# Two edits in a hybrid trunk kernel: a shorter ring of weight operands during the pooling branch, and decays and k ahead of the masked copies in the recurrence

## The chip, the cores and the metric

The kernel runs on one core of one Trainium2 chip. The metric is device time in microseconds (us). Five engines run side by side, each through its own queue in order: TensorE (PE; its weight loads are listed apart as PEld), VectorE (DVE), ScalarE (ACT), GpSimd (POOL) and SyncE (SP, which issues DMAs).

## The reference, cut to what matters

One layer over 2048 tokens of width 1024. The normalised input is projected; one part of the columns goes through a pooling mixer, one through a gated linear recurrence (HGRN2) with 4 heads of 128, both are projected, gated and merged, and a convolved, gated feed-forward layer follows.

```python
def hgrn2_mixer(zq, zf, zi, zo, lb, norm_g):
    q = jax.nn.silu(heads(zq))
    f = lbh + (1.0 - lbh) * jax.nn.sigmoid(heads(zf))
    k = 1.0 - f
    v = heads(zi)
    ...
        b = jnp.cumsum(gc, axis=2)
        diff = b[:, :, :, None, :] - b[:, :, None, :, :]
        decay = jnp.exp(jnp.where(causal[:, :, None], diff, -jnp.inf))
        attn = jnp.einsum('bhtk,bhtsk,bhsk->bhts', qc, decay, kc)
        o = (jnp.einsum('bhts,bhsv->bhtv', attn, vc)
             + jnp.einsum('bhtk,bhkv->bhtv', qc * jnp.exp(b), state))
    ...
xn = rmsnorm(x, norm1_g[l])
z = xn @ w_in[l]
ya = pool_mixer(u_pool, pool_w[l], pool_scale[l]) @ w_pa[l]
yb = hgrn2_mixer(zq, zf, zi, zo, lower_bounds[l], hgrn_norm_g[l]) @ w_pb[l]
x = x + (gates[:, :, 0] * ya + gates[:, :, 1] * yb) @ w_o[l]
x = x + conv_glu_ffn(rmsnorm(x, norm2_g[l]), w_up[l], conv_w[l], conv_b[l], w_down[l])
```

## The kernel before, in words

**Blocks and products.** Tokens are worked in two pairs of blocks of 512, so everything below happens twice: a mixer, then a feed-forward part, for the first 1024 tokens and again for the rest. The large projections use a scheme with seven products P1 to P7 in place of eight. A `Unit` runs them in the order P1, P2, P6, P5, P7, P4, P3 as far as its banks are concerned: P1 and P2 add into PSUM bank X, P6, P7 and P4 into Z, P5 and P3 into V. Between P6 and P7 the partial result in Z has to be read once: that is `u2` (line 1196), a DVE subtraction. P7 may start only when `u2` has read Z; between P7 and P4 stands `u3` (line 1200) in the same way. Each product is computed from operands split into a high and a low part, with three multiplies of 128 x 512 for each 128 rows, all recorded under line 148.

**The weight stream.** `Stream` loads weight tiles ahead (`load`), and `convert` splits one into high (line 231, ACT) and low (line 232, DVE) in a buffer `ops`, one of a ring of `N_OPS` = 6. In the first mixer POOL also forms sums of weight tiles (`comb`, line 444), which are stored and loaded again in the second mixer. `advance` is called once per tick, that is once in six multiplies, and converts the next operand if the program is not too far ahead: neither `room` (4 operands ahead of the one taken last) nor the ring (line 242) may be passed.

**The recurrence.** `hgrn_task` handles one head of one 512-token block; 16 such tasks run, as generators that three runners step forward between the multiplies of the projections. A task works a 128-token square by levels: widths 1 and 2 singly, then `two_levels(4)` and `two_levels(16)` (two widths each), then 64. At a level PE multiplies `k` by masked or scaled copies of `q` (`qm`) into a score bank `pl` (lines 1026 and 1066). DVE copies the valid parts of `pl` into `at` by masked copies (lines 1034 and 1037; 1073 and 1086 at widths 1 and 2), and multiplies `q` (1043), the decays `f` themselves (1045, 1046, 1049) and `k` (1047; 1094 at the single widths) for the next level. `two_levels` handles two halves of the tile, `i` = 0 and 2, each with its own `pl` bank, and one product L1047 scales all of `k`.

**Order.** The kernel emits its program in the order in which the generators step; a scheduler then sets the order on each engine, within the dependencies and the few that the kernel adds (`behind`, `in_turn`). So what stands where on an engine is read from the order of the built program, not from the code alone.

Of the kernel before, what the change touches and what calls it, by code (L numbers as in the profile page):

```python
# [15 lines left out]
ALU = mybir.AluOpType  # L16
AX = mybir.AxisListType

P = 128
# [11 lines left out]
NT = TB // P  # L31
# [44 lines left out]
N_OPS = 6  # L76
# [5 lines left out]
def tile_trunk(  # L82
# [60 lines left out]
    def join(task):  # L143
        while task.live:
            task.step()
# [22 lines left out]
    class Stream:  # L168
        def __init__(self):
            self.raws = []  # L170
            self.ops = []
            self.n_raw = 0
            self.tiles = []
            self.next = 0
            self.done = 0
            self.pins = {}
            self.stop = None
            self.room = LOOKAHEAD

        def raw(self, src, plus=None):  # L180
            r = Raw(src, plus)
# [57 lines left out]
        def advance(self, n):  # L239
            for _ in range(n):  # L240
                j = len(self.tiles)
                if j >= len(self.ops) or j == self.stop or j >= self.next + self.room or j - N_OPS >= self.done:
                    return
                self.convert()

# [34 lines left out]
    stream = Stream()  # L280
# [310 lines left out]
    masks = {}  # L591
# [373 lines left out]
    def hgrn_task(b, h, d, q, vd, zd, od):  # L965
# [23 lines left out]
        def mask(key, n):  # L989
            m = masks[key]  # L990
            return m.unsqueeze(1).to_broadcast([P, n, m.shape[1], m.shape[2]])

        def two_levels(hh):
            nb = P // (4 * hh)
            d5 = d.rearrange("p (c b t h) -> p c b t h", c=NT, t=4, h=hh)
            q5 = q.rearrange("p (c b t h) -> p c b t h", c=NT, t=4, h=hh)
            qv = q.rearrange("p (c b t h) -> p c b t h", c=NT, t=2, h=hh)
            av = att.rearrange("p (c b t h) -> p c b t h", c=NT, t=2, h=hh)
            av2 = att.rearrange("p (c b t h) -> p c b t h", c=NT, t=2, h=2 * hh)
            q2 = q.rearrange("p (c b t h) -> p c b t h", c=NT, t=2, h=2 * hh)  # L1000
            mvs = {}
            for i in range(0, NT, 2):
                cc = slice(i, i + 2)
                mv = (slot(f"qm{b}_{h}_{hh}_{i}")[:, :384]
                      .rearrange("p (c s x) -> p c s x", c=2, s=3))
                near = mv[:, :, 0].rearrange("p c (b h) -> p c b h", h=hh)
                half = mv[:, :, 1].rearrange("p c (b t h) -> p c b t h", t=2, h=hh)
                far = [mv[:, :, 1 + t].rearrange("p c (b h) -> p c b h", h=2 * hh)
                       for t in range(2)]
                act.copy(near, qv[:, cc, :, 1, :])  # L1010
                pool.tensor_copy(half[:, :, :, 0, :], q5[:, cc, :, 2, :])  # L1011
                dve.tensor_tensor(half[:, :, :, 1, :], q5[:, cc, :, 3, :],
                                  d5[:, cc, :, 2, 0:1].to_broadcast([P, 2, nb, hh]), ALU.mult)
                full = [P, 2, nb, 2 * hh]
                dve.tensor_tensor(far[1], far[0], d5[:, cc, :, 1, 0:1].to_broadcast(full),
                                  ALU.mult)
                dve.tensor_tensor(q2[:, cc, :, 1, :], far[1],
                                  d5[:, cc, :, 0, 0:1].to_broadcast(full), ALU.mult)
                mvs[i] = mv
            yield AHEAD  # L1020
            for i in range(0, NT, 2):
                cc = slice(i, i + 2)
                mv = mvs[i]
                pa_ = bank(f"pl{b}_{h}_{hh}_{i}", 384)
                for c in range(2):
                    ins = pe.matmul(pa_[:, c * 192 : c * 192 + 192],  # L1026
                                    ks[:, (i + c) * P : (i + c + 1) * P],
                                    mv[:, c].rearrange("p s x -> p (s x)"),
                                    start=True, stop=True)
                    if not (i or c):  # L1030
                        in_turn(ins)
                ps = pa_.rearrange("p (c s x) -> p c s x", c=2, s=3)
                yield 1
                dve.copy_predicated(av[:, cc, :, 1, :], mask(hh, 2),
                                    ps[:, :, 0].rearrange("p c (b h) -> p c b h", h=hh))
                for t in range(2):
                    dve.copy_predicated(av2[:, cc, :, 1, :], mask(8 * hh + 1 - t, 2),
                                        ps[:, :, 1 + t].rearrange("p c (b h) -> p c b h", h=2 * hh))
            dd = d.rearrange("p (b t h) -> p b t h", t=4, h=hh)
            qq = q.rearrange("p (b t h) -> p b t h", t=4, h=hh)  # L1040
            kk = ks.rearrange("p (b t h) -> p b t h", t=4, h=hh)
            nb *= NT
            dve.tensor_tensor(qq[:, :, 1, :], qq[:, :, 1, :],
                              dd[:, :, 0, 0:1].to_broadcast([P, nb, hh]), ALU.mult)
            dve.tensor_tensor(dd[:, :, 2, 0:1], dd[:, :, 2, 0:1], dd[:, :, 3, 0:1], ALU.mult)
            dve.tensor_tensor(dd[:, :, 1, 0:1], dd[:, :, 1, 0:1], dd[:, :, 2, 0:1], ALU.mult)
            dve.tensor_tensor(kk[:, :, 0:3, :], kk[:, :, 0:3, :],  # L1047
                              dd[:, :, 1:4, 0:1].to_broadcast([P, nb, 3, hh]), ALU.mult)
            dve.tensor_tensor(dd[:, :, 0, 0:1], dd[:, :, 0, 0:1], dd[:, :, 1, 0:1], ALU.mult)

        for lv in (0, 1, 2, 4, 6):
            hh = 1 << lv
            if lv in (2, 4):
                yield from two_levels(hh)
                continue
            nb = P // (2 * hh)
            qv = q.rearrange("p (c b t h) -> p c b t h", c=NT, t=2, h=hh)
            av = att.rearrange("p (c b t h) -> p c b t h", c=NT, t=2, h=hh)
            if lv < 2:
                qd, ad = ((q1, ae), (q2, ao))[lv]  # L1060
                if lv == 1:
                    act.copy(q2[:, :, 0].rearrange("p c (b h) -> p c b h", h=2), qv[:, :, :, 1, :])
                    yield AHEAD
                pa_ = bank(f"pl{b}_{h}_{hh}")
                for c in range(NT):
                    ins = pe.matmul(pa_[:, c * P : (c + 1) * P], ks[:, c * P : (c + 1) * P],
                                    qd[:, c].rearrange("p s x -> p (s x)"),
                                    start=True, stop=True)
                    if not c:
                        in_turn(ins)  # L1070
                yield 2
                pv4 = pa_.rearrange("p (c s x) -> p c s x", c=NT, s=2)
                dve.copy_predicated(ad, masks[-1 - lv].to_broadcast([P, NT, 64]), pv4[:, :, 1])
                pv4 = pv4[:, :, 0].rearrange("p c (b h) -> p c b h", h=hh)
# [10 lines left out]
            if lv < 2:  # L1085
                dve.copy_predicated(av[:, :, :, 1, :], mask(hh, NT), pv4)
            q3 = q.rearrange("p (b t h) -> p b t h", t=2, h=hh)
            k3 = ks.rearrange("p (b t h) -> p b t h", t=2, h=hh)
            d3 = d.rearrange("p (b t h) -> p b t h", t=2, h=hh)
            full = [P, NT * nb, hh]  # L1090
            if lv:
                dve.tensor_tensor(q3[:, :, 1, :], q3[:, :, 1, :],
                                  d3[:, :, 0, 0:1].to_broadcast(full), ALU.mult)
            dve.tensor_tensor(k3[:, :, 0, :], k3[:, :, 0, :],
                              d3[:, :, 1, 0:1].to_broadcast(full), ALU.mult)
            dve.tensor_tensor(d3[:, :, 0, 0:1], d3[:, :, 0, 0:1], d3[:, :, 1, 0:1], ALU.mult)
        yield 4
        pk = bank(f"pk{b}_{h}")
        for c in range(NT):
# [267 lines left out]
    def mixer(b0, forms, late):  # L1367
# [163 lines left out]
                add_forms(two, yf, k, f"yf{b0}", eng=dve)  # L1531

        join(mtask)
        otask = []

        def start_o(n):
# [4 lines left out]
        while any(t.live for t in runners):  # L1541
            for t in runners:
                if t.live:
                    t.step()
        join(otask[0])

        acc = {}

# [329 lines left out]
```

## Time and profile before

| what | value |
|---|---|
| median of 3 runs | 2533.51 us (2533.47 to 2534.64) |
| profiled execution | 2532.39 us |
| its span, first to last instruction | 2530.7 us |
| granted TensorE clock | 0.999 |
| PE busy | 2509.1 us (99%) |
| DVE busy | 1978.5 us (78%) |
| ACT busy | 1176.1 us (46%) |
| POOL busy | 753.4 us (30%) |

Durations in the prediction come from this profiled execution. In a row of the timeline the first number is the start in us from the span's start, the second the duration in us, then engine, line, operation, output and inputs (buffer numbers left out), shapes, and the count of equal rows run together; in brackets stands the idle time before it and what ended that. A row of the waits gives the waiting row, what it waited for, then the sum in us, the times, and the longest. In a row of the groups behind the bar stand the busy time in us and the mean of one in ns.

### The profile page before, as it was taken

How to read it: one execution, taken by the hardware profiler on the slowest of the kernel's cores; microseconds unless marked ns; L12 is line 12 of the kernel's file. 1: busy time of each engine (PE TensorE's matmuls, PEld its weight loads, DVE VectorE, ACT ScalarE, POOL GpSimd, SP SyncE). 2: the span in 40 equal slices, each digit the busy share in tenths (PEclk: the TensorE clock that was granted, in tenths of full speed). 3: DMA queues.
4: the chain of work that ended last, by engine and by line, in shares of the span. 5: the costliest groups of instructions: out<-in, count | busy, mean ns of one | idle time of the engine just before them, and what ended most of it. 6: DMA issues, size and time to landing. Idle time of an engine off the chain costs nothing.

```text
span 2530.7 us, 35649 instructions
## 1 busy us (share of the span) xinstructions
PE 2509.1 (99%) x11508; PEld 2053.6 (81%) x11508; DVE 1978.5 (78%) x3508; ACT 1176.1 (46%) x2218; POOL 753.4 (30%) x1127
## 2 busy tenths in 40 slices
PE   9999999999999999999999999999999999999998
PEld 7888888788888888888888888888888888888886
DVE  7889878598898777885596778765979888778755
ACT  6534343334555454554554343442355554445534
POOL 4344453003354334451320202200033432325410
PEclk9999999999999999999999999999999999999999
DMA  8878777777898879897344343446443454447852
GB/s 270 272 180 233 202 206 231 219 230 244 199 260 228 229 230 241 261 366 243 124 147 150 112 132 108 139 146 225 149 155 117 151 154 135 152 134 245 321 166 97
DMA packets 252332, 493.76 MB, mean 195 GB/s; under 512 B 26544, under 2 KB 43056, under 8 KB 251824
## 3 DMA queue, kind: packets, MB, share of 16 engines
q1 hardware_dynamic: 184512, 313.60, 39.1%
q0 software_dynamic: 42656, 112.74, 17.6%
q10 hardware_dynamic: 24976, 65.13, 7.6%
q8 instruction: 91, 1.49, 0.2%
q14 instruction: 97, 0.79, 0.1%
HBM read 381.79 MB, written 187.17 MB: 225 GB/s over the span
## 4 chain that ended last, share of the span: by engine, by line
PE 91%; DVE 5%; issue 1%; DMA 1%; POOL 1%; ACT 1%; SPq 0%; DVEq 0%; POOLq 0%; ACTq 0%
PE dn_P L148 16%; PE up_Z L148 14%; PE up_X L148 10%; PE up_V L148 10%; PE wo_P L148 6%; PE gr_Z L148 4%; PE pb L148 4%; PE pa L148 3%; PE io_Z L148 3%; PE gr_X L148 3%; PE fr_Z L148 2%; PE gr_V L148 2%; PE io_V L148 2%; PE fr_X L148 2%; PE fr_V L148 2%; PE pl L1026 1%
## 5 line engine op out<-in xcount | busy, mean ns | idle before, releaser
L231 ACT CAST ops<-raw 128x512 fp32r<-128x512 f32 x744 | 459.7, 620 | 817.8 <-PE dn_P L148 177.4
L232 DVE TENSOR_TENSOR ops<-raw,ops 128x512 fp32r<-128x512 f32 x744 | 553.0, 747 | 216.3 <-ACT ops L231 208.4
L1614 DVE SCALAR_TENSOR_TENSOR e<-h,cols,e 128x512 f32<-128x512 f32 x176 | 143.2, 818 | 30.9 <-ACT e L1612 26.3
L1612 ACT ACTIVATE e<-h,cols 128x512 f32<-128x512 f32 x176 | 142.3, 814 | 25.1 <-DVE h L1159 18.2
L1617 DVE SCALAR_TENSOR_TENSOR e<-h,cols,e 128x512 f32<-128x512 f32 x176 | 133.9, 770 | 2.5
L961 POOL DMA_DIRECT2D g_P<-dg_P x154 | 83.8, 545 | 160.3 <-PE dn_P L148 114.1
L1269 POOL TENSOR_TENSOR gf_P<-e,e 128x512 f32<-128x512 f32 x44 | 61.2, 1392 | 150.4 <-DVE e L1623 96.2
L1269 POOL TENSOR_TENSOR gf_P<-gf_P,e 128x512 f32<-128x512 f32 x44 | 59.1, 1344 | 72.0 <-DVE e L1623 71.5
L1409 POOL TENSOR_TENSOR q<-q,qs 128x512 f32<-128x512 f32 x16 | 21.7, 1357 | 185.2 <-ACT qs L1408 178.7
L1607 POOL COPY h<-h 128x2 f32<-128x2 f32 x88 | 40.8, 476 | 117.3 <-DVE h L1158 110.4
L1446 ACT ACTIVATE gt<-gt,cols 128x512 f32<-128x512 f32 x48 | 34.8, 725 | 86.8 <-DVE gt L1159 71.5
L1621 ACT ACTIVATE e<-e 128x512 f32<-128x512 f32 x88 | 55.6, 632 | 38.9 <-DVE e L1617 38.7
L1609 POOL COPY hist<-h 128x2 f32<-128x2 f32 x88 | 35.0, 398 | 117.6 <-DVE h L1159 115.8
L1159 DVE TENSOR_TENSOR h<-up_u,up_V 128x512 f32<-128x512 f32 x88 | 60.0, 682 | 10.2 <-PE up_V L148 9.7
L1244 DVE TENSOR_TENSOR x<-x,wo_P 128x512 f32<-128x512 f32 x88 | 56.0, 680 | 12.1 <-PE wo_P L148 11.9
L1244 DVE TENSOR_TENSOR ac<-ac,dn_P 128x512 f32<-128x512 f32 x72 | 47.1, 681 | 16.7 <-PE dn_P L148 16.5
L1011 POOL COPY qm<-q 128x64 f32<-128x64 f32 x64 | 29.9, 494 | 96.2 <-issue 25.9
L1026 PE MATMUL pl<-qm,k 128*128 128x192 f32 x256 | 50.6, 327 | 3.7 <-DVE k L1047 3.5
L1637 POOL DMA_DIRECT2D dg_P<-gf_P x88 | 50.7, 576 | 8.3 <-POOL gf_P L1269 7.4
L1607 POOL COPY h<-hist 128x2 f32<-128x2 f32 x88 | 45.0, 518 | 27.4 <-DVE m_T42l L657 27.3
L1194 ACT COPY up_e<-up_X 128x512 f32<-128x512 f32 x44 | 25.8, 586 | 58.2 <-PE up_X L148 53.1
L1026 PEld LDWEIGHTS pl<-qm,k 128*128 128x128 f32 x256 | 43.9, 189 | 9.6 <-POOL u L925 2.2
(1285 smaller groups left out, 8088.0 us busy)
## 6 DMA issues: line engine op xcount, KB each, us to landing
g_P<-dg_P POOLq DMA_DIRECT2D x154, 256.0 KB, 6.2
raw<-in_w_up_t SPq DMA_DIRECT2D x132, 256.0 KB, 3.2
raw<-in_w_in_t SPq DMA_DIRECT2D x98, 256.0 KB, 3.5
dg_P<-gf_P POOLq DMA_DIRECT2D x88, 256.0 KB, 4.0
dg_P<-e SPq DMA_DIRECT2D x66, 256.0 KB, 3.6
raw<-in_w_dn SPq DMA_DIRECT2D x66, 256.0 KB, 3.9
x<-in_x SPq DMA_DIRECT2D x64, 256.0 KB, 4.9
gd<-gt ACTq DMA_DIRECT2D x64, 256.0 KB, 3.2
```

The costliest lines, as they stand in the source:

```text
L148: count[1] = pe.matmul(*args, **kw)
L231: self.mark = act.copy(hi, v)
L232: low = self.low = dve.tensor_tensor(lo, v, f32(hi), ALU.subtract)
L961: eng.dma_start(t, d)
L1026: ins = pe.matmul(pa_[:, c * 192 : c * 192 + 192], ks[:, (i + c) * P : (i + c + 1) * P], mv[:, c].rearrange("p s x -> p (s x)"), start=Tru ...
L1159: return dve.tensor_tensor(dst, t, ps, ALU.add if how == "add" else ALU.subtract)
L1244: dve.tensor_tensor(t, t, ps[j], ALU.add if sg > 0 else ALU.subtract)
L1269: pin(eng.tensor_tensor(t, x0, x1, op))
L1607: pool.tensor_copy(h[:, 0:2], hist[:, mt] if hf == 0 else hs[s, 0][:, TB : TB + 2])
L1612: in_turn(act.activation(t, h[:, 2:], AF.Identity, bias=col(o_cb + mt), scale=col(o_cw + 4 * MF + mt)))
L1614: in_turn(second(dve.scalar_tensor_tensor(t, h[:, 1 : 1 + TB], col(o_cw + 2 * MF + mt), t, ALU.mult, ALU.add)))
L1617: dve.scalar_tensor_tensor(t, h[:, 0:TB], col(o_cw + mt), t, ALU.mult, ALU.add)
```

## The change: a shorter ring, and another order in the recurrence

There are two edits. The first makes the ring length a value of the stream and sets it to 5 in place of 6 from the end of the pooling tasks to the end of the pooling branch, with the drain of the recurrences behind it. The second is in `hgrn_task`. In `two_levels` the products of the decays and the remaining `q` product are emitted ahead of the score products, and the `k` product is cut into two halves, one behind each score product and ahead of all masked copies, which come together at the end. At widths 1, 2 and 64 the `k` product comes first, then `q` and the decays, then the masked copies, the larger one ahead of the diagonal one.

```diff
+            self.ring = N_OPS
...
-                if j >= len(self.ops) or j == self.stop or j >= self.next + self.room or j - N_OPS >= self.done:
+                if j >= len(self.ops) or j == self.stop or j >= self.next + self.room or j - self.ring >= self.done:
...
                 mvs[i] = mv
+            dd = d.rearrange("p (b t h) -> p b t h", t=4, h=hh)
+            qq = q.rearrange("p (b t h) -> p b t h", t=4, h=hh)
+            kk = ks.rearrange("p (b t h) -> p b t h", t=4, h=hh)
+            full = [P, NT * nb, hh]
+            dve.tensor_tensor(qq[:, :, 1, :], qq[:, :, 1, :],
+                              dd[:, :, 0, 0:1].to_broadcast(full), ALU.mult)
+            dve.tensor_tensor(dd[:, :, 2, 0:1], dd[:, :, 2, 0:1], dd[:, :, 3, 0:1], ALU.mult)
+            dve.tensor_tensor(dd[:, :, 1, 0:1], dd[:, :, 1, 0:1], dd[:, :, 2, 0:1], ALU.mult)
+            dve.tensor_tensor(dd[:, :, 0, 0:1], dd[:, :, 0, 0:1], dd[:, :, 1, 0:1], ALU.mult)
             yield AHEAD
+            pls = []
             for i in range(0, NT, 2):
...
-                ps = pa_.rearrange("p (c s x) -> p c s x", c=2, s=3)
+                pls.append(pa_.rearrange("p (c s x) -> p c s x", c=2, s=3))
                 yield 1
+                half = slice(i * nb, (i + 2) * nb)
+                dve.tensor_tensor(kk[:, half, 0:3, :], kk[:, half, 0:3, :],
+                                  dd[:, half, 1:4, 0:1].to_broadcast([P, 2 * nb, 3, hh]),
+                                  ALU.mult)
+            for i, ps in zip(range(0, NT, 2), pls):
+                cc = slice(i, i + 2)
                 dve.copy_predicated(av[:, cc, :, 1, :], mask(hh, 2),
                                     ps[:, :, 0].rearrange("p c (b h) -> p c b h", h=hh))
...
-            dve.tensor_tensor(qq[:, :, 1, :], qq[:, :, 1, :],
-                              dd[:, :, 0, 0:1].to_broadcast([P, nb, hh]), ALU.mult)
-            dve.tensor_tensor(dd[:, :, 2, 0:1], dd[:, :, 2, 0:1], dd[:, :, 3, 0:1], ALU.mult)
-            dve.tensor_tensor(dd[:, :, 1, 0:1], dd[:, :, 1, 0:1], dd[:, :, 2, 0:1], ALU.mult)
-            dve.tensor_tensor(kk[:, :, 0:3, :], kk[:, :, 0:3, :],
-                              dd[:, :, 1:4, 0:1].to_broadcast([P, nb, 3, hh]), ALU.mult)
-            dve.tensor_tensor(dd[:, :, 0, 0:1], dd[:, :, 0, 0:1], dd[:, :, 1, 0:1], ALU.mult)
...
-                dve.copy_predicated(ad, masks[-1 - lv].to_broadcast([P, NT, 64]), pv4[:, :, 1])
...
+            dve.tensor_tensor(k3[:, :, 0, :], k3[:, :, 0, :],
+                              d3[:, :, 1, 0:1].to_broadcast(full), ALU.mult)
             if lv:
                 dve.tensor_tensor(q3[:, :, 1, :], q3[:, :, 1, :],
                                   d3[:, :, 0, 0:1].to_broadcast(full), ALU.mult)
-            dve.tensor_tensor(k3[:, :, 0, :], k3[:, :, 0, :],
-                              d3[:, :, 1, 0:1].to_broadcast(full), ALU.mult)
             dve.tensor_tensor(d3[:, :, 0, 0:1], d3[:, :, 0, 0:1], d3[:, :, 1, 0:1], ALU.mult)
+            if lv < 2:
+                pv4 = pa_.rearrange("p (c s x) -> p c s x", c=NT, s=2)
+                dve.copy_predicated(av[:, :, :, 1, :], mask(hh, NT),
+                                    pv4[:, :, 0].rearrange("p c (b h) -> p c b h", h=hh))
+                dve.copy_predicated(ad, masks[-1 - lv].to_broadcast([P, NT, 64]), pv4[:, :, 1])
...
         join(mtask)
+        stream.ring = N_OPS - 1
...
         join(otask[0])
+        stream.ring = N_OPS
```

In the built program DVE has 3483 rows in place of 3451; PE, ACT, POOL and SP have as many as before. In the changed file the lines are shifted: the casts 231 and 232 are 232 and 233, the masked copies 1034 and 1037 are 1050 and 1053, the `q` products 1015, 1017 and 1043 are 1016, 1018 and 1025, the `f` products 1045, 1046 and 1049 are 1027, 1028 and 1029, `k` 1047 is 1045, the score product 1026 is 1036, `u2` 1196 is 1201. In the names the first number is the block of 512 tokens, the second the head, then the width and the half; the last is a count of buffers in the order in which the program made them.

DVE in the first mixer, from the second `k` product of head 0, block 1 to `u2` of unit ur0_0 (site 1 of the prediction), before:

```order
L1047 TENSOR_TENSOR k1_0_1467<-k1_0_1467,f1_0_1436 128x32x12
L232 TENSOR_TENSOR ops48_1780<-raw47_1333,ops48_1780 128x512
L1049 TENSOR_TENSOR f0_0_1390<-f0_0_1390 128x8
L1017 TENSOR_TENSOR q1_0_1364<-qm1_0_16_0_1759,f1_0_1436 128x4x32
L1017 TENSOR_TENSOR q1_0_1364<-qm1_0_16_2_1765,f1_0_1436 128x4x32
L1046 TENSOR_TENSOR f1_0_1436<-f1_0_1436 128x8
L1037 COPY_PREDICATED at0_0_1456<-m32_1036,pl0_0_4_2_1712 128x16x8
L1196 TENSOR_TENSOR ur0_0_u2_1791<-ur0_0_e1_1771,ur0_0_Z_1773 128x512
```

and now:

```order
L1045 TENSOR_TENSOR k1_0_1467<-k1_0_1467,f1_0_1436 128x16x12
L1050 COPY_PREDICATED at1_0_1470<-m4_957,pl1_0_4_2_1722 128x32x4
L1053 COPY_PREDICATED at0_0_1456<-m33_1080,pl0_0_4_2_1718 128x16x8
L1016 TENSOR_TENSOR qm1_0_16_2_1771<-qm1_0_16_2_1771,f1_0_1436 128x2x64
L1027 TENSOR_TENSOR f1_0_1436<-f1_0_1436 128x8
L233 TENSOR_TENSOR ops48_1790<-raw47_1333,ops48_1790 128x512
L1029 TENSOR_TENSOR f0_0_1390<-f0_0_1390 128x8
L1018 TENSOR_TENSOR q1_0_1364<-qm1_0_16_0_1765,f1_0_1436 128x4x32
L1201 TENSOR_TENSOR ur0_0_u2_1801<-ur0_0_e1_1781,ur0_0_Z_1783 128x512
L1053 COPY_PREDICATED at1_0_1470<-m33_1080,pl1_0_4_2_1722 128x16x8
L1053 COPY_PREDICATED at0_0_1456<-m32_1036,pl0_0_4_2_1718 128x16x8
```

The second half of `k1_0` now stands ahead of the copies out of `pl1_0_4_2`. One `q` product, one `f` product and the copy with mask `m32` out of `pl0_0_4_2` have gone from ahead of `u2` to behind it.

PE at the same place, the score products of width 16 of head 0 (`pl`) among the multiplies of unit ur0_0 (bank V is product P5, bank Z is P7), before:

```order
L148 MATMUL ur0_0_V_1793<-x1_T12h_765,ops45_1671 128x512
L1026 MATMUL pl0_0_16_0_1808<-qm0_0_16_0_1739,k0_0_1453 128x192 x2
L148 MATMUL ur0_0_V_1793<-x1_T13h_781,ops45_1671 128x512
L148 MATMUL ur0_0_V_1793<-x1_T13l_782,ops45_1671 128x512
L148 MATMUL ur0_0_V_1793<-x1_T13h_781,ops45_1671 128x512
L1026 MATMUL pl1_0_16_0_1811<-qm1_0_16_0_1759,k1_0_1467 128x192 x2
L1026 MATMUL pl0_0_16_2_1823<-qm0_0_16_2_1745,k0_0_1453 128x192 x2
L1026 MATMUL pl1_0_16_2_1829<-qm1_0_16_2_1765,k1_0_1467 128x192 x2
L148 MATMUL ur0_0_Z_1773<-x1_T30h_827,ops46_1701 128x512
```

and now, where the first `pl` stands three multiplies earlier:

```order
L1036 MATMUL pl1_0_16_0_1821<-qm1_0_16_0_1765,k1_0_1467 128x192 x2
L1036 MATMUL pl0_0_16_2_1831<-qm0_0_16_2_1748,k0_0_1453 128x192 x2
L148 MATMUL ur0_0_Z_1783<-x1_T30h_827,ops46_1709 128x512
L148 MATMUL ur0_0_Z_1783<-x1_T30l_828,ops46_1709 128x512
L148 MATMUL ur0_0_Z_1783<-x1_T30h_827,ops46_1709 128x512
L148 MATMUL ur0_0_Z_1783<-x1_T31h_846,ops46_1709 128x512
L148 MATMUL ur0_0_Z_1783<-x1_T31l_847,ops46_1709 128x512
L148 MATMUL ur0_0_Z_1783<-x1_T31h_846,ops46_1709 128x512
L148 MATMUL ur0_0_Z_1783<-x1_T32h_865,ops46_1709 128x512
L148 MATMUL ur0_0_Z_1783<-x1_T32l_866,ops46_1709 128x512
L1036 MATMUL pl1_0_16_2_1835<-qm1_0_16_2_1771,k1_0_1467 128x192 x2
L148 MATMUL ur0_0_Z_1783<-x1_T32h_865,ops46_1709 128x512
```

The last of the four `pl` groups has moved from ahead of P7 into it, behind eight of its twelve multiplies. PE's order moves at four places in all: here, at unit gr0_6 (there the last group moves the other way, from inside P7 to ahead of it), and by two or three multiplies at units ur2_0 and gr2_6 of the second mixer.

ACT where the ring is shorter, at the seam between the last gate unit and the pooling branch of the first mixer, before:

```order
L231 CAST ops131_4913<-raw97_4601 128x512
L656 CAST mxs1_0h_4816<-mx1_0_4814 128x512
L231 CAST ops132_4937<-raw98_4603 128x512
L1446 ACTIVATE gt0_1_7_4826<-gt0_1_7_4826,cols_84 128x512
L656 CAST mxs1_1h_4844<-mx1_1_4842 128x512
```

and now:

```order
L232 CAST ops131_4929<-raw97_4617 128x512
L657 CAST mxs1_0h_4832<-mx1_0_4830 128x512
L232 CAST ops132_4997<-raw98_4619 128x512
L1451 ACTIVATE gt0_1_7_4842<-gt0_1_7_4842,cols_84 128x512
L657 CAST mxs1_1h_4860<-mx1_1_4858 128x512
```

The program makes operand 132 later (its count grows by 60, its neighbours' by 16), and the cast stands where it stood.

More of the change, by code (lines that the diff above doesn't have):

```diff
@@ L1019, in two_levels @@
                 mvs[i] = mv
+            dd = d.rearrange("p (b t h) -> p b t h", t=4, h=hh)
[7 more added lines that the diff above has]
+            dve.tensor_tensor(dd[:, :, 0, 0:1], dd[:, :, 0, 0:1], dd[:, :, 1, 0:1], ALU.mult)
             yield AHEAD
+            pls = []
             for i in range(0, NT, 2):
-                cc = slice(i, i + 2)
                 mv = mvs[i]
@@ L1038, in two_levels @@
                                         ps[:, :, 1 + t].rearrange("p c (b h) -> p c b h", h=2 * hh))
[L1039 to L1042, printed above, removed]
-            dve.tensor_tensor(qq[:, :, 1, :], qq[:, :, 1, :],
-                              dd[:, :, 0, 0:1].to_broadcast([P, nb, hh]), ALU.mult)
-            dve.tensor_tensor(dd[:, :, 2, 0:1], dd[:, :, 2, 0:1], dd[:, :, 3, 0:1], ALU.mult)
-            dve.tensor_tensor(dd[:, :, 1, 0:1], dd[:, :, 1, 0:1], dd[:, :, 2, 0:1], ALU.mult)
-            dve.tensor_tensor(kk[:, :, 0:3, :], kk[:, :, 0:3, :],
-                              dd[:, :, 1:4, 0:1].to_broadcast([P, nb, 3, hh]), ALU.mult)
-            dve.tensor_tensor(dd[:, :, 0, 0:1], dd[:, :, 0, 0:1], dd[:, :, 1, 0:1], ALU.mult)
         for lv in (0, 1, 2, 4, 6):
@@ L1071, in hgrn_task @@
                 yield 2
-                pv4 = pa_.rearrange("p (c s x) -> p c s x", c=NT, s=2)
-                dve.copy_predicated(ad, masks[-1 - lv].to_broadcast([P, NT, 64]), pv4[:, :, 1])
-                pv4 = pv4[:, :, 0].rearrange("p c (b h) -> p c b h", h=hh)
             else:
@@ L1084, in hgrn_task @@
                 act.copy(av[:hh, :, 0, 1, :], pa_[:hh].rearrange("p (c h) -> p c h", c=NT))
-            if lv < 2:
-                dve.copy_predicated(av[:, :, :, 1, :], mask(hh, NT), pv4)
             q3 = q.rearrange("p (b t h) -> p b t h", t=2, h=hh)
```

## The prediction

> **What bounds the kernel now.** I read the page first (busy shares, the chain that ended last), then what TensorE (PE) waited for in the first mixer, then two stretches side by side, the recurrence of the first and of the second mixer, and last the rows around each PE wait.
>
> ```profile
> span 2530.7 us, 35649 instructions
> PE 2509.1 (99%) x11508; PEld 2053.6 (81%) x11508; DVE 1978.5 (78%) x3508; ACT 1176.1 (46%) x2218; POOL 753.4 (30%) x1127
> PE 91%; DVE 5%; issue 1%; DMA 1%; POOL 1%; ACT 1%; SPq 0%; DVEq 0%; POOLq 0%; ACTq 0%
> PE pl L1026 <- DVE k L1047: 3.5, 2, 1.8
> 118.00:425.00 307.00, 301.56 (x1534) 250.74 (x1533) 271.42 (x635) 120.09 (x276) 134.37 (x143) 1.00 0.80 217
> 1380.00:1680.00 300.00, 299.93 (x1540) 252.20 (x1539) 235.08 (x626) 122.85 (x277) 54.44 (x80) 1.00 0.40 121
> ```
>
> PE is busy 99% of the span and carries 91% of the chain, so the end moves only where PE waits or gets other work. The change adds no PE work. The last two rows (length, then busy time of PE, PEld, DVE, ACT, POOL, then the granted clock) say where a wait can be: in the first mixer's recurrence PE lacks 307.00 - 301.56 = 5.4 us, in the second 300.00 - 299.93 = 0.07 us. The clock is 1.00 in both. In the second the same rows move with the same cover, and I cost them at nothing; if that cover were gone, the prices below would hold there as well. The first row of the waits says what the change can aim at: twice PE's score product `pl` waits for `k` (L1047), 3.5 us together.
>
> **The ring: nothing.** In the order no row stands elsewhere because of it, on any engine, and no row waits for another one; the ACT rows shown above are where it acts, and they keep their places. What it could have touched is this wait at the seam to the pooling branch:
>
> ```profile
> 464.88 1.29 DVE L232 TENSOR_TENSOR ops<-raw,ops 128x512 fp32r<-128x512 f32 x2 [2.58 <-ACT ops L231]
> 466.09 1.12 DVE L1138 SCALAR_TENSOR_TENSOR ot<-po,ro,z 128x128 f32<-128x128 f32 x4
> 466.49 0.33 PE L1144 MATMUL pt<-ident,ot 128*128 128x128 f32 x1 [1.84 <-DVE ot L1138]
> ```
>
> Two weight subtractions (L232) stand ahead of `ot`, and PE waits 1.84 us for `ot`. They still stand there afterwards, so the 1.84 us stay. Cost 0, both ends.
>
> **The decays: prices.** Per pair of levels one `k` product over 384 columns becomes two over 192; 32 rows become 64. Steps are read from starts of rows that follow each other.
>
> ```profile
> L1047 DVE TENSOR_TENSOR k<-k,f 128x384 f32<-128x384 f32 x32 | 19.7, 616 | 0.0
> 154.48 0.48 DVE L1017 TENSOR_TENSOR q<-qm,f 128x128 f32<-128x128 f32 x2
> 154.89 0.16 DVE L1046 TENSOR_TENSOR f<-f 128x8 f32<-128x8 f32 x1
> 154.97 0.28 DVE L1037 COPY_PREDICATED at<-m,pl 128x128 f32<-128x128 uint8 x1
> 155.17 0.67 DVE L1196 TENSOR_TENSOR ur_u<-ur_e,ur_Z 128x512 f32<-128x512 f32 x1
> 158.63 0.54 DVE L1047 TENSOR_TENSOR k<-k,f 128x384 f32<-128x384 f32 x1
> 159.10 0.28 DVE L1034 COPY_PREDICATED at<-m,pl 128x128 f32<-128x128 uint8 x1
> ```
>
> A `q` product of 128 columns steps 0.41 / 2 = 0.20 us, a small `f` product 0.08, a masked copy 0.20, the full `k` 0.47. A half is not in the trace: it lies between 0.20 and 0.47, and on the line through 128 and 384 columns it is 0.27. Two halves cost 0.54 - 0.47 = 0.07 more than a full one, 32 x 0.07 = 2.2 us on DVE in all, hidden where DVE has slack (271 of 307, 235 of 300 us busy). Where it has none, position counts, and there are four such sites. The moved rows issue no DMA, and the rows of POOL and SP keep their order. On ACT three operand copies pass a gate's sigmoid and its store at two places of the second mixer; ACT is busy 122.85 of 300 us there, and no PE wait hangs on it, so that is 0.
>
> **Site 1**, unit ur0_0, the first wait for `k`:
>
> ```profile
> 151.85 0.40 PE L148 MATMUL ur_V<-x_T13h,ops 128*128 128x512 f32 x1
> 154.02 2.26 PE L1026 MATMUL pl<-qm,k 128*128 128x192 f32 x12 [1.77 <-DVE k L1047]
> 155.99 0.53 PE L148 MATMUL ur_Z<-x_T30h,ops 128*128 128x512 f32 x1
> 156.35 0.39 PE L148 MATMUL ur_Z<-x_T30l,ops 128*128 128x512 f32 x1
> 158.92 0.39 PE L148 MATMUL ur_X<-x_f4h,ops 128*128 128x512 f32 x1
> 150.08 1.31 POOL L444 TENSOR_TENSOR w51s<-raw,raw 128x512 f32<-128x512 f32 x1 [1.53 <-issue]
> 151.47 1.51 POOL L444 TENSOR_TENSOR w51s<-w51s,raw 128x512 f32<-128x512 f32 x1
> 150.13 1.29 DVE L1046 TENSOR_TENSOR f<-f 128x8 f32<-128x8 f32 x1
> 151.76 1.26 DVE L1045 TENSOR_TENSOR f<-f 128x8 f32<-128x8 f32 x1
> 153.33 0.55 DVE L1047 TENSOR_TENSOR k<-k,f 128x384 f32<-128x384 f32 x1
> ```
>
> The wait for `k` goes: the halves of `k1_0` stand ahead of the rows that PE then needs, and the first `pl` needs only the first half. But what is late next is already there. Behind the `pl` rows PE starts product P7 (`ur_Z<-x_T30h`, 155.99), which needs `u2` (L1196), and `u2` ran 155.17 + 0.67 = 155.84. It stands in DVE's queue behind all these rows, whichever order they have. After the change a `q` product (0.20), an `f` product (0.08) and a copy (0.20) stand behind it instead of ahead, and two `k` products are halved (+0.14): `u2` is 0.34 earlier. PE's order pays for it: the last `pl` of the four moves into P7 and splits it. Such a group takes 0.56 (414.40 to 414.96, below), and the first multiply behind it 0.36 where others take 0.23 (155.99 to 156.35), together 0.70. So with POOL's holds as they are, site 1 ends 0.70 - 0.34 = 0.36 **later**.
>
> The copies also free the score banks later. The last `pl` group waits for the copy `m32`, which now stands two copies (0.40) behind `u2`; eight multiplies of P7 (8 x 0.23 = 1.8 us) stand ahead of that group and cover it.
>
> The holds are the second half. `f` products of 8 columns took 1.29 and 1.26 us while POOL added weights (L444), 0.16 us otherwise: about 1.1 us lost each time. The new order puts other rows under POOL's sums. I take one hold fewer of the two, 0.36 - 1.1 = -0.74, since the `f` products of this stretch are spread wider; ends +0.36 (both stay) and -1.84 (both missed).
>
> The Trainium skill, "SBUF — State Buffer", section "SBUF: two separate sides", says that VectorE with two SBUF inputs and GpSimd take an exclusive lock for a whole instruction and the loser fully blocks. These rows agree. It also speaks against this change: `k` has two SBUF inputs, a masked copy reads its data from PSUM, so `k` put ahead of copies can hold up rows that would have run on. The trace has such a copy running free under a sum:
>
> ```profile
> 143.28 1.69 POOL L444 TENSOR_TENSOR w46s<-raw,raw 128x512 f32<-128x512 f32 x1 [6.96 <-DMA gd<-gt]
> 143.93 0.29 DVE L1037 COPY_PREDICATED at<-m,pl 128x128 f32<-128x128 uint8 x1
> ```
>
> **Site 2**, unit gr0_6, the second wait:
>
> ```profile
> 410.97 0.89 PE L1026 MATMUL pl<-qm,k 128*128 128x192 f32 x4 [1.77 <-DVE k L1047]
> 414.07 0.50 PE L148 MATMUL gr_Z<-x_T30h,ops 128*128 128x512 f32 x1
> 414.40 0.85 PE L1026 MATMUL pl<-qm,k 128*128 128x192 f32 x4
> 414.96 0.53 PE L148 MATMUL gr_Z<-x_T30l,ops 128*128 128x512 f32 x1
> 417.65 0.40 PE L148 MATMUL gr_X<-x_f4h,ops 128*128 128x512 f32 x1
> 409.12 1.29 POOL L444 TENSOR_TENSOR w121s<-w121s,raw 128x512 f32<-128x512 f32 x1
> 409.19 1.63 DVE L1047 TENSOR_TENSOR k<-k,f 128x384 f32<-128x384 f32 x1
> 413.34 0.67 DVE L1196 TENSOR_TENSOR gr_u<-gr_e,gr_Z 128x512 f32<-128x512 f32 x1
> ```
>
> Again P7 (414.07) starts when `u2` is done (413.34 + 0.67 = 414.01). Ahead of `u2` there are now one copy more (+0.20), one `f` fewer (-0.08) and two halved `k` (+0.14): 0.26 later, P7 at 414.33. Here the order helps PE: the last `pl` group moves from inside P7 to ahead of it, into the wait. P7 took 417.65 - 414.07 = 3.58 with it and takes 3.58 - 0.70 = 2.88 without: it ends at 417.21, -0.44. Ends: -1.5 if the 1.1 us hold on `k` (1.63 against 0.55) is missed, +0.66 if one comes on top.
>
> **Sites 3 and 4**, units gr0_2 and ur0_1, where PE comes to P7 just as `u2` ends or before:
>
> ```profile
> 233.09 0.68 DVE L1196 TENSOR_TENSOR gr_u<-gr_e,gr_Z 128x512 f32<-128x512 f32 x1
> 233.83 0.52 PE L148 MATMUL gr_Z<-x_T30h,ops 128*128 128x512 f32 x1
> 311.29 0.50 PE L148 MATMUL ur_Z<-x_T30h,ops 128*128 128x512 f32 x1 [1.11 <-DVE ur_u L1196]
> ```
>
> At both, three halves stand ahead of `u2` where one full `k` stood: 3 x 0.27 - 0.47 = 0.34 later, each straight onto PE. Ends 0 (a hold that swallows it) and +0.34.
>
> **Sum.** -0.74 - 0.44 + 0.34 + 0.34 = -0.50 us; ends -3.3 and +1.7. The profiled execution took 2532.39 us (span 2530.7, 1.69 around it), the median of the runs is 2533.51, 1.1 above it; I put the difference on the median: 2533.0, with 2530.2 to 2535.2 as its own range.
>
> **The rivals.** *The table is right*: the 3.5 us go and `u2` takes nothing of it. For it: the row of the waits says so. Against it: `u2` ends only 0.15 us and 0.06 us ahead of P7 at the two sites. Time 2533.5 - 3.5 = 2530.0. Chance 0.10.
>
> *Slower by the holds*: `k` ahead of the copies meets one of POOL's sums more at each of the four sites, and `u2` waits behind it. Price per site 1.1 us on the values with holds as today: (0.36 + 1.1) + (-0.44 + 1.1) + 2 x (0.34 + 1.1) = 5.0 us, 2538.5. It decides where a half `k` reaches DVE's head inside a sum while copies stand behind it. For it: the two holds at site 1 and the one at site 2. Against it: the sums start by their own loads and hits fall both ways. Chance 0.08. This is the mechanism on which the skill's rule stands.
>
> *Only half the change exists*: for the ring this is certain from the order and is in the sum; that the decays move nothing is excluded by the rows shown.
>
> **How the numbers follow.** Forecast 0.76, the table 0.10, the holds 0.08, something unseen 0.06, both ways alike. About 0.2% (5.1 us) is what a measurement of this kernel can tell from no change. Faster by that needs more than the whole first row of the waits: 0.03. Slower by that is about half of the second rival and the unseen part: 0.07. The range 2529.8 to 2536.0 takes in the forecast's own ends and the first rival and leaves out the second.
>
> **What would show it.** Right: no `pl <- k` among PE's waits; `u2` (L1201 then) named as what PE waits for at P7 of ur0_0, gr0_6, gr0_2 and ur0_1; `pt <- ot` still 1.8; 64 rows of `k` of 192 columns at about 0.35 us; PE's idle time in the first recurrence near 5 us, in the second under 0.3. Wrong: PE's idle time there under 2.5 us (the table was right), `k` halves of over 1 us in front of `u2` at several sites (the holds), or any new PE wait after 1380 us.

## The result: slower by about 3 us, and the profile after

| | before | changed |
|---|---|---|
| median of 18 runs, us | 2534.67 (2531.84 to 2538.18) | 2537.88 (2535.45 to 2541.02) |
| ratio | 1 | 1.0014, 95% interval 1.0008 to 1.0020 |
| profiled execution, us | 2532.39 | 2539.77 |
| PE idle in 118 to 425 us of the span | 5.4 | 9.3 |

The change costs 3.2 us at the medians, where 0.5 us of gain was forecast. The two profiled executions lie 7.4 us apart: that of before was 2.3 under its median, that of the changed kernel 1.9 over. So the rows below show where the time goes; how much goes there in the mean, the medians say.

The changed kernel's page, span and engines:

```profile
span 2538.0 us, 35650 instructions
PE 2512.8 (99%) x11508; PEld 2054.9 (81%) x11508; DVE 1986.4 (78%) x3540; ACT 1175.4 (46%) x2218; POOL 748.6 (29%) x1127
```

PE is busy 3.7 us longer with as many rows (2509.1 before); the rest of the 7.3 us between the spans is idle time. The windows of the two recurrences, with length and PE's busy time first and the granted clock third from the end:

```profile
118.00:425.00 307.00, 297.70 (x1495) 246.46 (x1494) 270.93 (x631) 117.55 (x270) 130.24 (x144) 0.99 0.77 211
1380.00:1690.00 310.00, 309.93 (x1587) 260.59 (x1586) 242.78 (x651) 128.19 (x287) 59.55 (x84) 1.00 0.40 122
```

The second recurrence is as full as before. Nearly the whole loss lies in the first. PE's lag, the start of a multiply less the start of the same multiply in the trace of before, is 0.5 us at 120 us, 7.0 at 430 and 7.4 at the end. In 118 to 425 us PE now lacks 307.00 - 297.70 = 9.3 us, and its clock is 0.99. What PE waited for there (118 to 470 us, the four largest; total, times, longest):

```profile
PE ur_Z L148 <- DVE ur_u L1201: 3.0, 2, 2.1
PE gr_Z L148 <- DVE gr_u L1201: 1.8, 2, 1.6
PE pl L1036 <- DVE qm L1016: 1.8, 2, 1.1
PE pl L1036 <- DVE at L1053: 1.3, 1, 1.3
```

Both waits for `k` (3.5 us) are gone. In their place PE waits for `u2` (L1201, 4.8 us), and, one step earlier in the same chain, for operands `qm` and for a masked copy `at` that frees a score bank.

The holds show in the groups of DVE rows in the first recurrence (after the bar: busy, mean ns of one). The `qm` and `q` products before:

```profile
L1017 DVE TENSOR_TENSOR q<-qm,f 128x128 f32<-128x128 f32 x32 | 8.9, 303 | 0.0
L1015 DVE TENSOR_TENSOR qm<-qm,f 128x128 f32<-128x128 f32 x32 | 8.4, 283 | 0.1
```

and in the changed kernel, as many rows of the same size:

```profile
L1016 DVE TENSOR_TENSOR qm<-qm,f 128x128 f32<-128x128 f32 x32 | 12.6, 409 | 0.1
L1018 DVE TENSOR_TENSOR q<-qm,f 128x128 f32<-128x128 f32 x32 | 10.8, 359 | 0.0
```

The dearest place is gr0_2, site 3. First DVE and POOL there in the kernel before:

```profile
225.22 0.68 DVE L1159 TENSOR_TENSOR gt<-gr_u,gr_V 128x512 f32<-128x512 f32 x1
...
226.29 1.60 DVE L232 TENSOR_TENSOR ops<-raw,ops 128x512 fp32r<-128x512 f32 x1
...
229.59 0.48 DVE L1017 TENSOR_TENSOR q<-qm,f 128x128 f32<-128x128 f32 x2
229.99 0.16 DVE L1046 TENSOR_TENSOR f<-f 128x8 f32<-128x8 f32 x1
230.07 0.49 DVE L1037 COPY_PREDICATED at<-m,pl 128x128 f32<-128x128 uint8 x2
230.47 1.05 DVE L1049 TENSOR_TENSOR f<-f 128x8 f32<-128x8 f32 x1
...
232.04 0.29 DVE L1037 COPY_PREDICATED at<-m,pl 128x128 f32<-128x128 uint8 x1
...
230.18 1.31 POOL L444 TENSOR_TENSOR w72s<-raw,raw 128x512 f32<-128x512 f32 x1 [0.91 <-issue]
231.57 1.70 POOL L444 TENSOR_TENSOR w72s<-w72s,raw 128x512 f32<-128x512 f32 x1
```

Then DVE, POOL and PE in the changed kernel:

```profile
227.42 0.67 DVE L1164 TENSOR_TENSOR gt<-gr_u,gr_V 128x512 f32<-128x512 f32 x1
...
229.35 1.12 DVE L1029 TENSOR_TENSOR f<-f 128x32 f32<-128x32 f32 x1
...
231.84 1.77 DVE L1018 TENSOR_TENSOR q<-qm,f 128x128 f32<-128x128 f32 x2
233.53 1.26 DVE L1028 TENSOR_TENSOR f<-f 128x8 f32<-128x8 f32 x1
234.71 0.48 DVE L1053 COPY_PREDICATED at<-m,pl 128x128 f32<-128x128 uint8 x2
...
235.99 0.34 DVE L1045 TENSOR_TENSOR k<-k,f 128x192 f32<-128x192 f32 x1
...
237.10 0.68 DVE L1201 TENSOR_TENSOR gr_u<-gr_e,gr_Z 128x512 f32<-128x512 f32 x1
...
231.69 1.56 POOL L445 TENSOR_TENSOR w72s<-raw,raw 128x512 f32<-128x512 f32 x1
233.33 1.44 POOL L445 TENSOR_TENSOR w72s<-w72s,raw 128x512 f32<-128x512 f32 x1
...
237.84 0.66 PE L148 MATMUL gr_Z<-x_T30h,ops 128*128 128x512 f32 x1 [1.62 <-DVE gr_u L1201]
238.30 0.63 PE L148 MATMUL gr_Z<-x_T30l,ops 128*128 128x512 f32 x1
...
241.28 0.47 PE L148 MATMUL gr_Z<-x_T32h,ops 128*128 128x512 f32 x1
```

POOL's two sums of `w72s` run in both. Before, the first met one product, an `f` (1.05 instead of 0.16); the `q` products were just done (230.07), and masked copies stood under the second sum and took their usual time. After, the first sum met the two `q` products (1.77 instead of 0.48) and the second an `f` product (1.26 instead of 0.16); the copies come when POOL is done. The `gt` row stands ahead of all these in both. With the other held row of each (1.60 for an unheld 0.68 before, 1.12 for 0.24 after), held time goes from 0.92 + 0.89 = 1.81 us to 0.88 + 1.29 + 1.10 = 3.27 us. Those 1.46 us put `u2` back, and so do three halves of `k` where one full one stood (3 x 0.27 - 0.47 = 0.34). DVE had come to this stretch 2.2 us later already (`gt`: 225.22 before, 227.42 now): 2.2 + 1.46 + 0.34 = 4.0, and `u2` stands at 237.10 instead of 233.09. P7 follows it, 237.84 instead of 233.83. PE's multiplies ahead of it lag 1.5 us behind those of before, so the lag rises by 2.5 us at this one row: the 1.46, the 0.34, and the 0.7 by which DVE came later than PE. What made DVE come later was not traced.

Then something follows that no sum had: from 238.30 to 241.28 PE's multiplies stand 0.43 us apart, not 0.23. The windows around it (clock third from the end):

```profile
236.00:238.00 2.00, 0.38 (x3) 0.16 (x2) 1.93 (x9) 0.00 (x0) 1.30 (x1) 1.00 1.10 202
238.00:240.00 2.00, 2.00 (x5) 1.52 (x6) 2.00 (x10) 0.00 (x0) 0.00 (x0) 0.51 1.06 260
240.00:242.00 2.00, 2.00 (x7) 1.62 (x6) 2.00 (x11) 0.00 (x0) 0.00 (x0) 0.64 1.05 396
```

Behind two us with 0.38 us of work PE is granted half its clock for about 3.4 us. Seven steps at 0.43 for 0.23 cost 1.4 us more. The Trainium skill, "TensorE: Matmul & The Clock Gate", section "Part 1: The HAM clock gate", has half the clock after an idle window of about 3.4 us, and the full clock again after about 3.4 us of work. The length of the slow stretch agrees, but here a shorter gap with one `pl` group in it was enough.

### The profile page after: what moved, and what is told of

It is laid out like the page before. It is cut to its first block, busy times and chain, and to the rows that moved or that the text cites. A ratio compares the mean times of both kernels' runs of the same rounds, so it can differ in the third digit from the quotient of the medians.

```text
span 2538.0 us, 35650 instructions
## 1 busy us (share of the span) xinstructions
PE 2512.8 (99%) x11508; PEld 2054.9 (81%) x11508; DVE 1986.4 (78%) x3540; ACT 1175.4 (46%) x2218; POOL 748.6 (29%) x1127
## 4 chain that ended last, share of the span: by engine, by line
PE 90%; DVE 6%; issue 1%; DMA 1%; ACT 1%; POOL 1%; SPq 0%; DVEq 0%; POOLq 0%; ACTq 0%
PE dn_P L148 16%; PE up_Z L148 14%; PE up_X L148 10%; PE up_V L148 10%; PE wo_P L148 6%; PE gr_Z L148 4%; PE pb L148 4%; PE pa L148 3%; PE io_Z L148 3%; PE gr_X L148 2%; PE fr_Z L148 2%; PE gr_V L148 2%; PE io_V L148 2%; PE fr_X L148 2%; PE fr_V L148 1%; DVE ops L233 1%
```

## The experiments

Each ratio is to the kernel before on the same chip (its medians there 2534.84, 2534.02 and 2534.04 us for e1 to e4, e5 to e8 and e9 to e10). The last column is PE's idle time in 118 to 425 us of the one profiled execution, 307.00 less PE's busy time.

| kernel | median, us | ratio (95%) | PE idle, us |
|---|---|---|---|
| before | 2534.67 | 1 | 5.4 |
| e9 ring alone | 2534.47 | 1.0000 (0.9991 to 1.0009) | 5.6 |
| e10 decays only | 2533.81 | 0.9998 (0.9989 to 1.0007) | 6.0 |
| e4 two levels, `k` whole | 2534.74 | 1.0001 (0.9992 to 1.0010) | 7.5 |
| e7 single levels | 2535.42 | 1.0005 (0.9996 to 1.0014) | 7.5 |
| e8 two levels, `k` halved | 2536.07 | 1.0009 (1.0000 to 1.0018) | 7.8 |
| e1 all decays | 2538.34 | 1.0013 (1.0004 to 1.0022) | 8.5 |
| changed kernel | 2537.88 | 1.0014 (1.0008 to 1.0020) | 9.3 |
| e2 before, no sums | 2523.77 | 0.9964 (0.9950 to 0.9978) | 1.8 |
| e3 changed, no sums | 2522.10 | 0.9954 (0.9942 to 0.9967) | 1.0 |
| e6 before, sums on DVE | 2522.40 | 0.9957 (0.9944 to 0.9969) | 1.0 |
| e5 changed, sums on DVE | 2522.03 | 0.9959 (0.9946 to 0.9973) | 0.9 |

**Which half of the change: e1 and e9.** e1 is the changed kernel without the two assignments of `stream.ring`; e9 is the kernel before with them.

```diff
@@ e1, against the changed kernel
-        stream.ring = N_OPS - 1
...
-        stream.ring = N_OPS
@@ e9, against the kernel before
+        stream.ring = N_OPS - 1
...
+        stream.ring = N_OPS
```

> The decay edit without the ring edit. On all engines its rows stand in the order of the changed kernel. My theory (the ring does nothing, the decays do all): the time of the changed kernel, 1.0014 of before (about 3 us, 2 to 4.5), and PE waits again for u2 at gr0_2 and ur0_1. Rival (the ring has a share): within 1 us of before, or more than 1.5 us from the changed kernel. Second question: the profiled run of the changed kernel lost 4.1 us at gr0_2, 1.46 of it at half the clock; if that is typical and not one run's luck, this profile shows a stretch of about 3.4 us at half the clock there as well.

> The ring edit without the decay edit. Every row and wait stands as in the kernel before. Theory: 1.000 of before, within 1 us. Rival (the ring has a share in the 3.2 us): 1.5 us or more slower. Second question: this profile is a second look at the order of before. If which DVE row a sum of POOL meets is a matter of a few tenths of a us, it shows a wait of 1 to 2 us for u2 at gr0_2 or other stretched rows than the first profile of before, which was 1.1 us under the median; if the holds of before are fixed by its order, the same two waits for k of 1.8 us appear.

The ring does nothing that e9 can tell (its interval is some 2 us either way), and the decays alone make the loss. e9 also shows how firm a profile of this kernel is: its order is that of before, yet one of the two waits for `k` has become a wait for POOL's `u`, and its lag wanders between -0.5 and 0.9 us. e1's longest wait for `u2`:

```profile
PE gr_Z L148 <- DVE gr_u L1201: 1.8, 2, 1.6
```

Windows of e1, the recurrence and a short one near its end:

```profile
118.00:425.00 307.00, 298.51 (x1499) 248.22 (x1498) 271.85 (x642) 117.49 (x270) 129.76 (x144) 0.99 0.78 213
417.00:419.00 2.00, 2.00 (x7) 2.00 (x8) 2.00 (x11) 0.00 (x0) 0.00 (x0) 0.54 0.59 190
```

Waits of `pl` in e9:

```profile
PE pl L1027 <- POOL u L926: 1.5, 1, 1.5
PE pl L1027 <- DVE k L1048: 1.4, 1, 1.4
```

Held rows at gr0_2, the first two in e1, the last in e9:

```profile
231.32 1.76 DVE L1018 TENSOR_TENSOR q<-qm,f 128x128 f32<-128x128 f32 x2
233.00 1.26 DVE L1028 TENSOR_TENSOR f<-f 128x8 f32<-128x8 f32 x1
...
230.20 1.04 DVE L1050 TENSOR_TENSOR f<-f 128x8 f32<-128x8 f32 x1
```

In e1 PE waits again up to 1.6 us for `u2`; its lag behind the trace of before rises by 2.5 us at P7 of gr0_2, as in the changed kernel, and the same rows are held there. e9 holds the same `f` there as before, and its lag does not rise. That part is no accident of one run. The half clock is: here it is at gr0_6 (0.54 in 417 to 419) and not at gr0_2, so it has no fixed place. At ur0_1 e1 loses 0.3 us where the changed kernel lost 1.4.

**Are the holds the cause: e2 and e3.**

```diff
-            pool.tensor_tensor(t, x0, x1, ALU.add)
+            act.copy(t, x0)
```

> The kernel before, where the 56 sums of two weight blocks that POOL forms for the projections of the first mixer are replaced by a copy of one of the two on ACT (so the second block is left out of the sum). POOL then holds up no DVE row there by a sum. Holds theory: the stretched f products (1.29 and 1.26 us) and the stretched k at gr0_6 (1.63 us) are gone, both 1.8 us waits of PE for k shrink to under 0.9 us each, and the kernel is 2 to 4 us faster than before. Rival (the order alone makes the waits): waits of PE for k stay at 3 us or more together and the time is within 1 us of before.

> The same replacement in the changed kernel. Holds theory: the 3.2 us between the changed kernel and before are mostly holds and the half clock behind them, so against the kernel before with the same replacement this one is no more than 1 us slower (by the queue positions 0.36 - 0.44 + 0.34 + 0.34 = 0.6 us), and no stretch at half the clock shows in the recurrence. Rival (the queue ahead of u2 is longer, whatever POOL does): still 2.5 us or more slower than that kernel.

The one wait of PE that e2 has left between 118 and 470 us:

```profile
PE gr_Z L148 <- DVE gr_u L1196: 1.7, 1, 1.7
```

e2's window of the recurrence:

```profile
118.00:425.00 307.00, 305.25 (x1566) 256.54 (x1565) 240.49 (x640) 151.40 (x332) 62.16 (x95) 1.00 0.79 219
```

The same of e3, the wait and the window:

```profile
PE gr_Z L148 <- DVE gr_u L1201: 1.0, 1, 1.0
```

```profile
118.00:425.00 307.00, 305.96 (x1569) 257.18 (x1569) 241.51 (x656) 152.22 (x333) 65.33 (x95) 1.00 0.80 221
```

With no sums on POOL the loss is gone: the changed order is 1.7 us faster at the medians, not 3.2 slower. Whether it gains is not shown, since the five runs of each overlap (2520.96 to 2524.26 against 2522.81 to 2527.26). The waits for `k` of before are gone too: they hung on POOL's sums as well. DVE is some 30 us less busy in this stretch (240.49 for 271.42) with as many rows on it: rows are shorter. The exclusive lock that the Trainium skill, "SBUF — State Buffer", section "SBUF: two separate sides", describes agrees with that. And e2 is 11 us faster than before, where 2 to 4 were expected: POOL's sums cost this kernel far more than the waits for `k` showed. One more wait that goes with them, in all four kernels without sums on POOL, is the 1.8 us of `pt` for `ot` at the seam. How much of the gain is held DVE rows, and how much is POOL itself being free earlier (in e9 PE waits 1.5 us for POOL's `u`), these runs do not separate. ACT's rows and a few of PE's stand in another order than in the originals, in e2 and e3 alike.

**Without leaving work out: e5 and e6.**

```diff
-            pool.tensor_tensor(t, x0, x1, ALU.add)
+            dve.tensor_tensor(t, x0, x1, ALU.add)
```

> The changed kernel with POOL's 56 weight sums of the first mixer's projections moved to DVE (nothing is left out). On DVE a sum is one more row of 128x512, some 0.6 us where POOL takes 1.3, and it can no longer hold up another DVE row. Holds theory: DVE is 241 us busy in 118 to 425 without the sums and gains about 45 x 0.6 = 27, so it stands near the 272 of today but without holds; PE idles under 3 us there (8.5 and 9.3 us in the two profiles of the changed order), and the kernel is 4 to 11 us faster than before. Rival (DVE is full and any row ahead of u2 costs its length on PE): each sum pushes u2 back by 0.6 us at several units, the kernel is not faster than the changed one (2538) or slower.

> The same move of the sums to DVE in the kernel before. Holds theory: also 3 to 10 us faster than before, and the changed order with its sums on DVE is within 1 us of it or up to 2 us faster, as without sums (2522.10 against 2523.77). Rival (the decay order itself costs 3 us): the changed order stays 3 us slower than this kernel.

e5's window of the recurrence:

```profile
118.00:425.00 307.00, 306.10 (x1566) 256.60 (x1565) 267.58 (x703) 125.33 (x283) 66.64 (x94) 1.00 0.79 219
```

Its rows at gr0_2:

```profile
228.04 0.67 DVE L1201 TENSOR_TENSOR gr_u<-gr_e,gr_Z 128x512 f32<-128x512 f32 x1
228.64 0.68 DVE L445 TENSOR_TENSOR w70s<-w65s,raw 128x512 f32<-128x512 f32 x1
232.08 0.53 PE L148 MATMUL gr_Z<-x_T30h,ops 128*128 128x512 f32 x1
```

e6's window of the recurrence:

```profile
118.00:425.00 307.00, 305.98 (x1566) 256.76 (x1565) 267.96 (x688) 125.66 (x283) 64.39 (x95) 1.00 0.79 219
```

DVE does the sums itself, 48 of the 56 in this stretch, and is still no busier than before (267.96 for 271.42 us): 0.6 us for a sum (228.04 to 228.64 is the step of a row of this size) is no more than the sums cost it as holds, (271.42 - 240.49) / 48 = 0.64 us. `u2` is done 3.4 us before PE needs it (228.71 against 232.08). Both kernels are 12 us faster than before, and between them the change is worth nothing that these runs can tell (2522.03 and 2522.40; 2521.97 to 2524.58 and 2521.73 to 2523.42). The sums on DVE are the version to keep, with either order.

**Which part of the decays: e10, e4, e7, e8.** e10 moves only the `q` and `f` products of the two-level part. e4 adds to it one whole `k` ahead of the copies. e8 is the two-level part as changed. e7 is the single-level part alone, on the kernel before.

```diff
@@ e10 and e4, two levels, against the changed kernel
-                dve.tensor_tensor(kk[:, half, 0:3, :], kk[:, half, 0:3, :],
-                                  dd[:, half, 1:4, 0:1].to_broadcast([P, 2 * nb, 3, hh]),
-                                  ALU.mult)
@@ e4 ahead of the loop of copies, e10 behind all copies
+            dve.tensor_tensor(kk[:, :, 0:3, :], kk[:, :, 0:3, :],
+                              dd[:, :, 1:4, 0:1].to_broadcast([P, NT * nb, 3, hh]), ALU.mult)
@@ e10 alone: the copies behind each score product again
-            for i, ps in zip(range(0, NT, 2), pls):
+                ps = pls[-1]
@@ e10, e4, e8, single levels as before: copies ahead of these again
             dve.tensor_tensor(k3[:, :, 0, :], k3[:, :, 0, :],
                               d3[:, :, 1, 0:1].to_broadcast(full), ALU.mult)
@@ e7, against the kernel before: these, and the q and f products, ahead of the copies
             dve.tensor_tensor(k3[:, :, 0, :], k3[:, :, 0, :],
                               d3[:, :, 1, 0:1].to_broadcast(full), ALU.mult)
```

> Of the decay edit only the q and f products of the two-level part ahead of the score products; k whole and behind the copies, the single-level part as before. On DVE six rows change places. Theory (k ahead of the copies and its cutting make the loss, with the holds): within 1 us of before, 1.000. Rival (the decays ahead make it): 2 us or more slower.

> Of the decay edit only the two-level part, and k as one product over 384 columns behind both score products and ahead of the masked copies (not two halves); the single-level part stays as before. At gr0_2 and ur0_1 the rows ahead of u2 stand then as in the kernel before: no k product between the copies and u2. If the second half of k ahead of u2 makes the loss at these two sites: no loss there, total within -1.5 to +0.7 us of before. If k ahead of the copies costs wherever it stands: 2.5 us or more slower, like the changed kernel.

> Of the decay edit only the single-level part (widths 1, 2 and 64: k, q and f ahead of the masked copies). The rows ahead of u2 at gr0_2 and ur0_1 stand as in the kernel before. Theory (the second half of k and the holds it meets make the loss): 0 to +1 us against before, no wait for u2 at gr0_2 beyond before's. Rival (the single-level part carries the loss): +2.5 us or more.

> Of the decay edit only the two-level part, with k in two halves as in the changed kernel; the single-level part as before. Theory: nearly the whole loss, +2 to +4 us against before, with a wait of PE for u2 of 1 us or more at gr0_2. Against the variant with k whole (+0.1 us, 2534.74 beside 2534.84) the cutting of k is then the cost. Rival (the loss comes only from both parts together): within 1 us of before.

No part alone is shown to carry the loss. At the medians the decays ahead cost nothing and so does `k` whole ahead of the copies; the two-level part with `k` in halves costs 2.1 us and the single levels 1.4. The last two add up to the loss, but each of their intervals touches or holds no change, and they overlap with that of e4. Against the expectation e7 does lose at gr0_2, where its DVE rows ahead of `u2` are those of before:

```profile
230.29 1.61 DVE L1017 TENSOR_TENSOR q<-qm,f 128x128 f32<-128x128 f32 x2
231.82 1.26 DVE L1046 TENSOR_TENSOR f<-f 128x8 f32<-128x8 f32 x1
...
230.24 1.31 POOL L444 TENSOR_TENSOR w72s<-raw,raw 128x512 f32<-128x512 f32 x1 [0.26 <-issue]
```

POOL's first sum starts here 0.05 us ahead of the `q` products (230.24, 230.29); before, it started 0.6 us behind them (230.18, 229.59) and met the copies and one `f`. DVE being 0.7 us later at this place is enough: same rows, same sums, other rows held. So the rows just ahead of `u2` do not fix the holds there; what stands further up the queue shifts which rows the sums meet.

How far PE's lag behind the trace of before rises at P7 of gr0_2, one trace each:

| kernel | `k` and the copies | rise, us |
|---|---|---|
| e9, e10 | all `k` behind the copies | 0.0, 0.0 |
| e4, e8 | `k` of the two levels ahead | 1.4, 1.4 |
| e7 | `k` of the single levels ahead | 2.0 |
| e1, changed kernel | both ahead | 2.5, 2.5 |
| e2, e3, e5, e6 | no sums on POOL | 0.0 each |

Every trace with sums on POOL and some `k` ahead of the copies loses at this place, and no other does. At the medians the 1.4 us of e4 do not show; its interval is wide enough to hold them.

## Why the prediction was wrong

**Ring, second recurrence, `pt`: right.** The ring has no effect that e9 can tell, the second recurrence is full, and among PE's waits `pt` still waits 1.8 us for `ot`:

```profile
PE pt L1149 <- DVE ot L1143: 1.8, 1, 1.8
```

**The waits for `k` go, `u2` takes their place: right.** None of PE's waits is `pl` for `k`, and "the table is right" is excluded. `u2` is what PE waits for at three of the four sites; at gr0_6 it is a masked copy one step earlier (1.3 us). That the chain behind `k` was the real bound was the right reading.

**Site 1, "one hold fewer", -0.74: wrong.** Two rows are held there as before, now an `f` (1.29) and a `qm` product (1.34). The end "both stay", +0.36, was right: over this unit the lag behind the trace of before rises by 0.4 us, and by 0.2 in e1.

**Sites 3 and 4, +0.34 each with ends 0 and +0.34: the step that failed.** gr0_2 measured 2.5 us (2.5 in e1) and 1.5 more while the clock was low, ur0_1 1.4 (0.3 in e1). I had priced only the longer queue there and let the holds stand where they were; at gr0_2 the held time rose by 1.46 us, from 1.81 to 3.27. The upper end should have had a hold more, 1.1 us each, as the second rival did. What made the 1.4 us at ur0_1 was not traced. Site 2 measured -0.9 in the changed kernel, where -0.44 was forecast, and +1.2 in e1, where the half clock fell on it.

**The rivals.** "Slower by the holds", 2538.5, came nearest, with a chance of 0.08. Its place was half right. Its sign was halves of `k` of over 1 us ahead of `u2` at several sites; there was one, at gr0_6, which lost nothing over the unit:

```profile
417.43 1.06 DVE L1045 TENSOR_TENSOR k<-k,f 128x192 f32<-128x192 f32 x1
```

Elsewhere it was `q`, `qm` and `f` products that were held, and the dearest of them at gr0_2. My argument against it, that hits fall both ways, did not hold at gr0_2. One reason could be that the change is not symmetric. Masked copies run free under a sum (230.07 to 232.04 before), so a queue that alternates products with copies hides part of each sum behind copies; the change gathers the products together and the copies behind them. That the loss hangs on POOL's sums is shown by e2 and e3, and by e5 and e6. That it is not the chance of one execution at gr0_2 is shown by the table above. That this gathering is the reason is only argued from the rows, and e7 speaks against it at this place: there its products alternate with copies as before, and it loses 2.0 us.

**The size.** 3.2 us at the medians is under the 0.2% that I had called the bound; with 18 runs each, the interval 1.0008 to 1.0020 still lies wholly above 1, so the loss is real. The range ended at 2536.0 because it left out this rival.

What stays open: which step further up the queue brings the sums onto other rows at gr0_2; how the 3.2 us at the medians split between sites, since each profile is one execution; and how often the half clock falls.

## What to carry to other kernels

A wait table names the last row ahead of a wait, not what made it late: both waits for `k` went away when POOL's sums did, and a reordering of DVE that ignores those sums just moves them onto other rows. Where a small row of one engine shows two durations a fixed step apart (0.16 and 1.26 us here), price the other engine's instruction as time on this one before deciding who runs it: 56 sums at 0.6 us on DVE were cheaper than at 1.3 us or more on POOL. And where an estimate takes holds as given at one site and as chance at another, give both sites both ends.

## What the hardware showed that I had not expected

PE's clock fell to half for about 3.4 us behind waits of 1.6 to 2.2 us: 0.51 and 0.64 in 238 to 242 of the changed kernel, 0.54 in 417 to 419 of e1. The profiles of e8 and e10 have one such stretch each in the first recurrence, that of e7 one at its end (470 to 474, behind `pt`); those of before, e2 to e6 and e9 have none there, though before has three waits of about 1.8 us. It adds some 1.4 us to a long wait, at a place that changes from run to run.
